# Two query heads mixed in one product in the sliding-window layer of a two-layer decoder

## The chip, the core and the metric

The kernel runs on one core of a Trainium2 chip. The core has a matrix engine (TensorE, PE in the profile; its weight loads are a row of their own, PEld), a vector engine (VectorE, DVE), a scalar engine (ScalarE, ACT), GpSimd (POOL) and a queue that issues transfers (SyncE, SP). Products of PE land in PSUM, which here is used as eight banks of 128 x 512 numbers of 32 bits; ACT and DVE read them from there. The metric is the device time in microseconds of one execution of the whole program: the median over runs, with a profiled execution beside it.

## What is computed

The reference is a decoder trunk of two layers over 512 tokens of width 1024. Layer A is multi-head latent attention with a squared-ReLU MLP; layer B, which the change touches, is sliding-window attention with 16 query heads that share 4 key and value heads, learned sinks and a bias by distance, again with an MLP. Cut to layer B's attention:

```python
def _swa(x, w_q, sinks, w_o, k_band, v_band, rel_bias):
    q = (x @ w_q).reshape(B, nb, BLOCK, SWA_KV_HEADS, G, SWA_HEAD_DIM)
    s = jnp.einsum('bnqkgd,bnjkd->bnkgqj', q, k_band).astype(jnp.float32) * SWA_HEAD_DIM ** -0.5
    ...
    s = jnp.where(mask[None, :, None, None], s + bias, -jnp.inf)
    ...
    m = jnp.maximum(s.max(-1), sink)
    p = jnp.exp(s - m[..., None])
    denom = p.sum(-1) + jnp.exp(sink - m)
    p = (p / denom[..., None]).astype(x.dtype)
    o = jnp.einsum('bnkgqj,bnjkd->bnqkgd', p, v_band).reshape(B, S, SWA_Q_HEADS * SWA_HEAD_DIM)
    return o @ w_o
```

The window is 128 tokens and tokens are handled in 4 blocks of 128, so the queries of a block see the keys of their own block and of the one before: 256 keys, and 128 for the first block.

## The kernel before, in words

**Numbers in two parts.** Each 32-bit number is split into a high part that the fast product format holds exactly and a low rest (`split`, L75: an ACT copy makes the high part at L77, a subtraction on DVE or on another engine makes the low one at L80). Most products are three matmuls: high by high, high by low, low by high (`three`, L108). Where a head is only 64 wide, the high part stands in 64 of the 128 rows and the low part in the other 64, and one matmul does both. `group` (L102) issues such a list into one PSUM bank, so nearly all matmuls carry line L104. PE instructions, and the transfers of SP, are kept in program order (`pe`, L85). Where the instructions of ACT, DVE and POOL stand in their queues, and which PSUM bank or buffer a tile gets, is settled by the framework when the program is built.

**PSUM.** `bank()` (L66) hands out one of 6 banks for products, `tbank()` one of 2 for transposes. A bank comes free when all that reads it is done.

**The steps of layer B.** `run_steps` (L508) walks over the 16 heads. In step u it issues, in this order: the scores of head u + 2 (`AHEAD_B` is 2), pieces of filling work, the turning of head u, and then `mix`, here that of head u - 1 (per 1, lag 1, L1327).

- `scores` (L1224): 8 matmuls into two banks; DVE adds the bias and takes the maximum in four pieces (L1247), turns that into the exponent's offset (L1251); ACT makes four exponentials (L1255) and that of the sink (L1259); DVE sums and inverts; POOL scales the weights `p` (L1262, L1264). The two banks stay taken until the exponentials have read them, the first bank until the second exponential, the second until the fourth.
- filling work: half of a product of queries (`queries`, L1204: 12 matmuls of 512 columns, one bank for the two halves of a pair of heads; evacuated into `q` by ACT at L1218 and DVE at L1219), or a part of the output product w_so (`proj.part`, L457: 6 matmuls of 512 columns; the three token blocks each hold a bank of their own until the product is finished). In steps 1 to 10 a step has one half product of queries: odd steps begin one and take a bank, even steps end it. The list at L1317 gives for each part of w_so its token block t, its piece kp of the sum and the step u in which it is issued.
- `turn` (L1267): 7 transposes of `p` into two transpose banks (L1275, L1277), split into `pth` and `ptl`, of which two buffers each exist.
- `mix` (L1288): the values times the turned weights, for the 4 key blocks, high and low: 8 matmuls, six of 256 columns and two of 128, into one bank. The bank's upper 64 rows hold what the low part of the values gives: ACT copies them to `low` (L1304), DVE adds them to the lower 64 rows into one half of `o` (L1305). After the second head of a pair the pair's `o` is split into `oh` (ACT) and `ol` (POOL), which the output product reads.

After the last step `run_steps` issues what is left of the filling work and the last mix; then `proj.finish` (L467) issues the parts of w_so that are not done, in the order of kp and then t, and the second half of the output columns with the layer norm. The second layer's MLP follows.

Which work stood in which step follows from the list and the shares of filling work in `run_steps` (S scores, Q query half, so(t,kp) part of w_so, T turn, M mix):

```
step 9:  S11 Q T9 M8            step 13:  S15 so(1,0) T13 M12
step 10: S12 Q T10 M9           step 14:  so(1,1) so(2,0) T14 M13
step 11: S13 so(0,0) so(0,1) T11 M10   step 15:  so(2,1) so(0,2) T15 M14
step 12: S14 T12 M11            end:      so(1,2) M15, then finish
```

Of the kernel before, what the change touches and what calls it, by code (L numbers as in the profile page):

```python
# [15 lines left out]
P = 128  # L16
# [32 lines left out]
def build(tc, nc, io, out):  # L49
    with ExitStack() as top:  # L50
# [456 lines left out]

        def run_steps(units, ahead, scores, turn, mix, fill, per, lag, rest):  # L508

            total = sum(f[0] for f in fill)
            n, spent, at = len(units), 0.0, 0
            for u in range(-ahead, n):
                if u + ahead < n:
                    scores(*units[u + ahead])
                target = total * (u + ahead + 1) / (n + ahead)
                while at < len(fill) and (spent < target or fill[at][1] <= u) and fill[at][2] <= u:
                    fill[at][3]()
                    spent += fill[at][0]  # L520
                    at += 1
                if u < 0:
                    continue
                turn(*units[u])
                if u >= lag and (u - lag) % per == per - 1:
                    mix(units[u - lag][0])
            for f in fill[at:]:
                f[3]()
            for f in rest:
                f()  # L530
            for u in range(n, n + lag):
                if (u - lag) % per == per - 1:
                    mix(units[u - lag][0])

# [630 lines left out]
        with tc.tile_pool(name="swa", bufs=1) as mp:  # L1165
# [55 lines left out]
            ps_of = [None] * SQH  # L1221
            pts = [None] * SQH

# [43 lines left out]
            def turn(h, _):  # L1267
                p = ps_of[h]
                pth = mp.tile([P, NT, 256], F32R, tag="pth", bufs=2, name=nm("pth"))
                ptl = mp.tile([P, NT, 256], F32R, tag="ptl", bufs=2, name=nm("ptl"))  # L1270
                for k2 in range(2):
# [8 lines left out]
                    else:  # L1280
                        flat = lambda z: z.rearrange("p a b -> p (a b)")
                        c = slice(512, 512 + 384)
                        split(flat(pth)[:, c], flat(ptl)[:, c], flat(pt)[:, 0:384])
                pts[h] = pth, ptl

            ob = [None] * 8

            def mix(h):  # L1288
                m, a, j = h // 2, h % 2, h // GRP
                if a == 0:  # L1290
                    ob[m] = mp.tile([P, S], F32, tag="o", bufs=2, name=nm("o"))
                o = ob[m]
                pth, ptl = pts[h]

                b = bank()
                for kb in range(NT):
                    w = 256 if kb + 1 < NT else P
                    group(
                        b[:, kb * P : kb * P + w],
                        [(vv[:, kb, j, :], pth[:, kb, :w]), (vv[:, kb, j, :], ptl[:, kb, :w])],  # L1300
                        kb == 0, kb == NT - 1, skip_group_check=True,
                    )
                low = mp.tile([64, S], F32, tag="low", bufs=2, name=nm("low"))
                nc.scalar.activation(low, b[hi, :], AF.Copy)  # L1304
                nc.vector.tensor_add(o[(lo, hi)[a], :], b[lo, :], low)  # L1305
                if a == 1:
                    split(oh[m // 4][:, m % 4, :], ol[m // 4][:, m % 4, :], o, nc.gpsimd)

            proj = TokMajor(Pair(oh, ol), add_scaled_last, "w_so")
            fill = []  # L1310
            for m in range(2, 8):
                for part in range(2):
                    fill.append((2.6, 2 * m - AHEAD_B - 3 + part, -9, lambda m=m, part=part: queries(m, part)))
                if m == 2:
                    for t in range(1, NT):
                        fill.append((2.6, 0, -9, lambda t=t: values(t)))
            for t, kp, u in ((0, 0, 11), (0, 1, 11), (1, 0, 13), (1, 1, 14), (2, 0, 14), (2, 1, 15), (0, 2, 15), (1, 2, 16)):  # L1317
                fill.append((1.3 if t < 2 else 0, u, u, lambda t=t, kp=kp: proj.part(t, kp)))
# [7 lines left out]
            values(0)  # L1326
            run_steps([(h, 0) for h in range(SQH)], AHEAD_B, scores, turn, mix, fill, 1, 1, [])  # L1327

# [116 lines left out]
```

## Time and profile before

| | |
|---|---|
| median of 3 runs | 1007.86 us (1007.84 to 1008.55) |
| the profiled execution's own time | 1009.88 us |
| its span in the profile | 1008.0 us |
| mean granted PE clock over the span | 0.996 |
| busy share of the span: PE, PEld, DVE, ACT, POOL | 98%, 89%, 76%, 55%, 21% |

The profile's times are those of one execution, from the start of its span. A row of a view by groups gives an engine, a line of the kernel, the operation, the tile written and the tiles read, the shape, the count, busy time and the mean length of one. A row of the timeline gives the start, the length, the engine and the instruction; in square brackets stands how long the engine had been idle and what ended that. Matmuls overlap, so that the distance of two starts, and not the length of one, is what a matmul costs; the names of the two operands in a matmul's row do not follow a fixed order. The chain of waits is followed back from the last instruction. Layer B's attention runs from about 521 us to 650 us of the span.

### The profile page before, as it was taken

What the parts mean: (1) busy time and instruction counts of PE and PEld (TensorE: products, weight loads), DVE (VectorE), ACT (ScalarE), POOL (GpSimd) and SP (SyncE); (2) the same over time, 40 slices, a digit from 0 to 9 for tenths busy, and PEclk for the clock granted to TensorE, in tenths of its full rate; (3) what the DMA queues carried; (4) which work ended last, traced back from release to release, by engine and by line L of the source; (5) the groups of instructions that cost most, each with busy time, mean ns of one, the idle gap of its engine ahead of it and who ended that gap; (6) DMA issues with size and microseconds to landing.
All of it is one profiled execution on the core that took longest, in us unless ns stands there. A gap on an engine that the chain in (4) does not pass through costs nothing.

```text
span 1008.0 us, 15943 instructions
## 1 busy us (share of the span) xinstructions
PE 991.8 (98%) x6172; PEld 895.1 (89%) x6172; DVE 770.6 (76%) x1236; ACT 555.0 (55%) x851; POOL 216.1 (21%) x203
## 2 busy tenths in 40 slices
PE   8999999999999999999999999999999999999997
PEld 8888888998999999998899988889898999998986
DVE  5588866998669768877686778698886886898756
ACT  5456653457537637646146688446663754665620
POOL 0231101122212211310003664212122032122000
PEclk9999999999999999999999999999999999999999
DMA  6431136389978986973232212258697798798432
GB/s 245 135 100 50 63 105 210 92 176 236 165 167 219 178 188 194 228 123 129 80 105 96 84 64 74 84 167 195 179 200 175 167 215 168 168 269 147 108 101 84
DMA packets 60247, 149.56 MB, mean 148 GB/s; under 512 B 5211, under 2 KB 9740, under 8 KB 60172
## 3 DMA queue, kind: packets, MB, share of 16 engines
q0 software_dynamic: 24320, 58.73, 33.0%
q1 hardware_dynamic: 35852, 89.82, 26.4%
q8 instruction: 49, 0.80, 0.3%
q14 instruction: 26, 0.21, 0.1%
HBM read 146.41 MB, written 4.22 MB: 149 GB/s over the span
## 4 chain that ended last, share of the span: by engine, by line
PE 95%; ACT 2%; DVE 1%; DMA 1%; issue 1%; SPq 0%; DVEq 0%; ACTq 0%
PE mm L104 87%; PE tr L104 5%; DMA xraw<-in_xT 1%; PE tr L1105 1%; PE tr L647 1%; ACT p L1255 1%; ACT wh L77 1%; PE tr L1275 1%; PE tr L1277 0%; PE tr L427 0%; ACT q L1218 0%; DVE fac L80 0%; ACT pth L77 0%; PE mm L1035 0%; PE tr L899 0%
## 5 line engine op out<-in xcount | busy, mean ns | idle before, releaser
L104 PE MATMUL mm<-wh,fac 128*128 128x512 f32 (+1 forms) x944 | 293.0, 387 | 2.4 <-DVE fac L80 2.3
L77 ACT ACTIVATE wh<-wq 128x1024 fp32r<-128x1024 f32 x164 | 173.5, 1060 | 193.6 <-PE mm L104 135.8
L80 DVE TENSOR_TENSOR wl<-wq,wh 128x1024 fp32r<-128x1024 f32 x164 | 199.5, 1220 | 74.2 <-ACT wh L77 73.4
L104 PE MATMUL mm<-xth,wh 128*128 128x256 f32 (+1 forms) x944 | 246.8, 289 | 0.7 <-ACT p L1255 0.7
L104 PE MATMUL mm<-xth,wl 128*128 128x256 f32 (+1 forms) x816 | 236.1, 289 | 0.0
L104 PEld LDWEIGHTS mm<-wh,fac 128*128 128x128 f32 x944 | 176.1, 188 | 39.0 <-DVE fac L80 3.8
L104 PE MATMUL mm<-xtl,wh 128*128 128x256 f32 (+1 forms) x688 | 199.9, 291 | 0.0
L104 PE MATMUL mm<-wl,fac 128*128 128x512 f32 (+1 forms) x472 | 182.3, 386 | 0.0
L104 PEld LDWEIGHTS mm<-xth,wh 128*128 128x128 f32 x944 | 171.7, 192 | 4.0 <-ACT p L1255 1.5
L104 PEld LDWEIGHTS mm<-xth,wl 128*128 128x128 f32 x816 | 156.3, 192 | 2.0
L77 ACT ACTIVATE wh<-raw 128x1024 fp32r<-128x1024 f32 (+4 forms) x85 | 84.8, 998 | 97.6 <-PE mm L104 65.0
L104 PEld LDWEIGHTS mm<-xtl,wh 128*128 128x128 f32 x688 | 131.8, 192 | 2.4
L199 POOL DMA_DIRECT2D wq<-in_up x64 | 77.5, 1228 | 262.0 <-DVE wl L80 192.1
L80 DVE TENSOR_TENSOR wl<-raw,wh 128x1024 fp32r<-128x1024 f32 (+3 forms) x65 | 76.8, 1188 | 37.7 <-ACT wh L77 37.6
L104 PEld LDWEIGHTS mm<-wl,fac 128*128 128x128 f32 x472 | 88.8, 188 | 16.7
L199 POOL DMA_DIRECT2D wq<-in_down x48 | 42.0, 875 | 188.3 <-DVE wl L80 181.2
L80 POOL TENSOR_TENSOR wl<-raw,wh 128x1024 fp32r<-128x1024 f32 (+2 forms) x20 | 41.4, 2075 | 86.4 <-ACT wh L77 83.9
L104 PE MATMUL mm<-wh,oh 128*128 128x512 f32 x128 | 51.0, 399 | 0.9 <-ACT p L1255 0.9
L104 PE MATMUL mm<-wh,ol 128*128 128x512 f32 x128 | 50.3, 393 | 0.0
L104 PE MATMUL mm<-wl,oh 128*128 128x512 f32 x128 | 50.1, 391 | 0.0
L387 POOL TENSOR_TENSOR rs<-mv,half 128x1 f32<-128x1 f32 x16 | 10.0, 623 | 168.6 <-DVE mv L408 168.5
L553 DVE TENSOR_TENSOR x<-mm,x 128x512 f32<-128x512 f32 (+1 forms) x49 | 32.9, 674 | 15.5 <-PE mm L104 15.5
(217 smaller groups left out, 1847.2 us busy)
## 6 DMA issues: line engine op xcount, KB each, us to landing
wq<-in_up POOLq DMA_DIRECT2D x64, 512.0 KB, 8.5
wq<-in_down POOLq DMA_DIRECT2D x48, 512.0 KB, 6.3
wq<-in_up SPq DMA_DIRECT2D x32, 512.0 KB, 7.1
raw<-in_down SPq DMA_DIRECT2D x28, 512.0 KB, 6.8
wq<-in_down SPq DMA_DIRECT2D x24, 512.0 KB, 5.9
raw<-in_up SPq DMA_DIRECT2D x16, 512.0 KB, 4.8
raw<-in_w_o SPq DMA_DIRECT2D x8, 512.0 KB, 4.1
raw<-in_w_sq SPq DMA_DIRECT2D x8, 512.0 KB, 3.3
```

What stands on the lines that cost most here:

```text
L77: high = nc.scalar.activation(dst_h, src, AF.Copy)
L80: low = (engine or nc.vector).tensor_sub(dst_l, src, f32(dst_h))
L104: pe(nc.tensor.matmul(dst, st, mv, start=first and i == 0, stop=last and i == len(pairs) - 1, **kw))
L199: nc.gpsimd.dma_start(half(a, jp), chunk(*more, jp), accum_op=ALU.add)
L387: nc.gpsimd.tensor_tensor(r, v, half, ALU.pow)
L553: nc.vector.tensor_add(xs[t][:, c], b, xs[t][:, c])
L647: pe(nc.tensor.transpose(pt[:, a, :], xs[t][:, k * P : (k + 1) * P], ident))
L1105: pe(nc.tensor.transpose(pt[:, kb * P : (kb + 1) * P], p[:, kb * P : (kb + 1) * P], ident))
L1255: nc.scalar.activation(p[:, n, lo_c:], bs[n // 2][:, n % 2, lo_c:], AF.Exp, bias=nb[:, n : n + 1], scale=SWA_SCALE, accum_out=sm[:, n : n ...
L1275: pe(nc.tensor.transpose(pt[:, a, 0:P], p[:, kb, P:256], ident))
```

## The change

In layer B the unit of mixing becomes the pair of heads. The turned weights of both heads of a pair stand side by side in one tile, `[P, 2, NT, 256]`, for `pth` and for `ptl`, with one buffer each in place of two of half the size. `mix` handles the pair at once, for two halves of the tokens: for the first 256 tokens key blocks 0 and 1, for the last 256 key blocks 1, 2 and 3, with the columns of both heads in one matmul: 512 columns where it was 256 per head, 256 where it was 128. Key block 1 is cut in two at the token half. Each half has its own bank, in which the two heads lie side by side, its own ACT copy, and two additions on DVE, one for each head. `run_steps` is told per 2 and lag 1, so that a mix stands in every even step from 2 on and one after the last step, and `mix_first`, by which it stands ahead of the turning in its step. Layer A calls `run_steps` as before, without `mix_first`.

The list of parts of w_so is another one. By the same rules as above the steps become:

```
step 9:  S11 Q T9               step 13:  S15 so(1,0) so(1,1) T13
step 10: S12 Q M(8,9) T10       step 14:  so(0,2) so(1,2) M(12,13) T14
step 11: S13 so(0,0) T11        step 15:  so(2,0) so(2,1) T15
step 12: S14 so(0,1) M(10,11) T12   end:  so(2,2) M(14,15), then finish
```

```diff
-        def run_steps(units, ahead, scores, turn, mix, fill, per, lag, rest):
+        def run_steps(units, ahead, scores, turn, mix, fill, per, lag, rest, mix_first=False):
+            def mixes(u):
+                if u >= lag and (u - lag) % per == per - 1:
+                    mix(units[u - lag][0])
...
+                if mix_first:
+                    mixes(u)
                 turn(*units[u])
-                if u >= lag and (u - lag) % per == per - 1:
-                    mix(units[u - lag][0])
+                if not mix_first:
+                    mixes(u)
...
             for u in range(n, n + lag):
-                if (u - lag) % per == per - 1:
-                    mix(units[u - lag][0])
+                mixes(u)
...
-            pts = [None] * SQH
+            pts = [None] * (SQH // 2)
...
-                pth = mp.tile([P, NT, 256], F32R, tag="pth", bufs=2, name=nm("pth"))
-                ptl = mp.tile([P, NT, 256], F32R, tag="ptl", bufs=2, name=nm("ptl"))
+                if h % 2 == 0:
+                    pts[h // 2] = [
+                        mp.tile([P, 2, NT, 256], F32R, tag=tag, bufs=1, name=nm(tag)) for tag in ("pth", "ptl")
+                    ]
+                pth, ptl = (z[:, h % 2] for z in pts[h // 2])
...
             def mix(h):
-                m, a, j = h // 2, h % 2, h // GRP
-                if a == 0:
-                    ob[m] = mp.tile([P, S], F32, tag="o", bufs=2, name=nm("o"))
-                o = ob[m]
-                pth, ptl = pts[h]
-
-                b = bank()
-                for kb in range(NT):
-                    w = 256 if kb + 1 < NT else P
-                    group(
-                        b[:, kb * P : kb * P + w],
-                        [(vv[:, kb, j, :], pth[:, kb, :w]), (vv[:, kb, j, :], ptl[:, kb, :w])],
-                        kb == 0, kb == NT - 1, skip_group_check=True,
-                    )
-                low = mp.tile([64, S], F32, tag="low", bufs=2, name=nm("low"))
-                nc.scalar.activation(low, b[hi, :], AF.Copy)
-                nc.vector.tensor_add(o[(lo, hi)[a], :], b[lo, :], low)
-                if a == 1:
-                    split(oh[m // 4][:, m % 4, :], ol[m // 4][:, m % 4, :], o, nc.gpsimd)
+                m, j = h // 2, h // GRP
+                o = mp.tile([P, S], F32, tag="o", bufs=2, name=nm("o"))
+                for i, blocks in enumerate((((0, 0, 256), (1, 0, P)), ((1, P, 256), (2, 0, 256), (3, 0, P)))):
+                    b = bank().rearrange("p (a b) -> p a b", a=2)
+                    for kb, c0, c1 in blocks:
+                        at = kb * P + c0 - i * 256
+                        group(
+                            b[:, :, at : at + c1 - c0], [(vv[:, kb, j, :], z[:, :, kb, c0:c1]) for z in pts[m]],
+                            kb == i, kb == 2 * i + 1, skip_group_check=True,
+                        )
+                    low = mp.tile([64, 2, 256], F32, tag="low", bufs=2, name=nm("low"))
+                    nc.scalar.activation(low, b[hi, :, :], AF.Copy)
+                    for a, rows in enumerate((lo, hi)):
+                        nc.vector.tensor_add(o[rows, i * 256 : (i + 1) * 256], b[lo, a, :], low[:, a, :])
+                split(oh[m // 4][:, m % 4, :], ol[m // 4][:, m % 4, :], o, nc.gpsimd)
...
-            for t, kp, u in ((0, 0, 11), (0, 1, 11), (1, 0, 13), (1, 1, 14), (2, 0, 14), (2, 1, 15), (0, 2, 15), (1, 2, 16)):
+            for t, kp, u in ((0, 0, 11), (0, 1, 12), (1, 0, 13), (1, 1, 13), (0, 2, 14), (1, 2, 14), (2, 0, 15), (2, 1, 15), (2, 2, 16)):
...
-            run_steps([(h, 0) for h in range(SQH)], AHEAD_B, scores, turn, mix, fill, 1, 1, [])
+            run_steps([(h, 0) for h in range(SQH)], AHEAD_B, scores, turn, mix, fill, 2, 1, [], True)
```

2 lines of the change are left out of this document (removed).

## The prediction, made before the changed kernel was seen

> **What bounds the kernel now.** I read the page first (shares, chain), then the chain and PE's timeline in layer B, and the windows and groups there for what could take PE's place.
>
> ```profile
> PE 95%; ACT 2%; DVE 1%; DMA 1%; issue 1%; SPq 0%; DVEq 0%; ACTq 0%
> ```
>
> PE carries 95% of the chain, so the change is worth what it takes from PE's queue: products, and PE's waits. The chain over one pair of heads shows the wait of a middle step:
>
> ```profile
> 586.78 4.41 PE mm L104 x27
> ...
> 591.21 0.68 ACT wh L77
> ...
> 592.29 0.59 ACT q L1218
> 592.88 0.23 ACT pth L77
> 593.11 0.15 issue
> 593.26 0.91 ACT p L1255 x4
> ```
>
> An odd step's filling part wants a bank; it starts at 594.21, when ACT has made the second exponential of the head before; ACT came to it through a weight split, a query copy and a turned copy. The same rows of PE's timeline show what it costs, and what matmuls cost:
>
> ```profile
> 587.50 0.27 PE L104 MATMUL mm<-skh,q 128*128 128x128 f32 x1
> 588.72 0.40 PE L104 MATMUL mm<-xtl,wh 128*128 128x512 f32 x1
> 591.01 0.39 PE L104 MATMUL mm<-xth,wl 128*128 128x512 f32 x1
> 592.12 0.28 PE L104 MATMUL mm<-ptl,vv 128*128 128x256 f32 x1
> 592.72 0.22 PE L104 MATMUL mm<-pth,vv 128*128 128x128 f32 x1
> 592.89 0.27 PE L104 MATMUL mm<-skh,q 128*128 128x128 f32 x1
> 593.75 0.28 PE L104 MATMUL mm<-skl,q 128*128 128x256 f32 x1
> 594.21 0.50 PE L104 MATMUL mm<-xth,wh 128*128 128x512 f32 x1 [0.18 <-ACT p L1255]
> 594.55 0.39 PE L104 MATMUL mm<-xtl,wh 128*128 128x512 f32 x1
> ```
>
> From start to start: ten of 512 columns take 591.01 - 588.72 = 2.29, **0.229 us** each; five of 256 take 592.72 - 592.12, **0.12** each; the two of 128 take 0.17, **0.085** each. The wait: 594.21 comes 0.46 after a matmul that takes 0.12, and the next start 0.34 after one that takes 0.23: 0.34 + 0.11 = **0.45 us**. The chain shows this wait at 571.76, 582.98, 594.21, 605.45 and 616.67, in steps 3 to 11, once in a pair: 2.25 us.
>
> Steps 12 and 13, where step 12 has no filling work, are worse:
>
> ```profile
> 621.18 0.27 PE L104 MATMUL mm<-skh,q 128*128 128x128 f32 x1
> 624.21 0.28 PE L104 MATMUL mm<-skl,q 128*128 128x256 f32 x1
> 625.31 0.39 PE L104 MATMUL mm<-skh,q 128*128 128x256 f32 x1 [0.83 <-DVE o L1305]
> 625.53 0.28 PE L104 MATMUL mm<-skl,q 128*128 128x256 f32 x1
> 625.77 0.28 PE L104 MATMUL mm<-skl,q 128*128 128x256 f32 x1
> 626.74 0.50 PE L104 MATMUL mm<-wh,oh 128*128 128x512 f32 x1 [0.69 <-ACT p L1255]
> 627.07 0.40 PE L104 MATMUL mm<-wl,oh 128*128 128x512 f32 x1
> ```
>
> Head 15's scores wait for a bank until the addition into `o` (1.10 from start to start, less 0.12: 0.98, and 0.10 behind it), then so(1,0) until an exponential (0.97 - 0.12 = 0.85, and 0.10): **2.03 us**. Right behind follows this, in windows (length, busy us and count of PE, PEld, DVE, ACT, POOL, then PE's granted clock):
>
> ```profile
> 587.00:598.20 11.20, 11.02 (x72) 9.71 (x71) 8.63 (x30) 9.56 (x30) 7.30 (x6) 1.00 0.21 76
> 624.40:627.80 3.40, 1.88 (x10) 1.43 (x10) 3.19 (x10) 3.35 (x13) 1.82 (x2) 1.00 0.01 2
> 627.80:631.20 3.40, 3.40 (x16) 3.11 (x15) 1.88 (x9) 2.06 (x6) 2.73 (x3) 0.50 0.00 0
> ```
>
> For 3.40 us in which PE was busy 1.88 the clock was full, and for the next 3.40 it was half: **1.7 us** lost. ACT, in a middle pair, is busy 9.56 of 11.20 us, DVE 8.63: neither is the bound, but both are queues full enough to be late.
>
> **Products.** A pair costs 12 x 0.12 + 4 x 0.085 = 1.78 us before. After, key blocks 0 and 2 are 4 matmuls of 512 columns, key block 1 is 4 of 256 as before, key block 3 is 2 of 256: 4 x 0.229 + 6 x 0.12 = 1.64. That is 0.14 a pair, and 8 pairs give **-1.15 us** (48 matmuls and as many weight loads fewer). Most of it is key block 3 (0.34 to 0.24). No row shows a moving operand of two stretches; I price it by columns, and the bound from the other side is two 256s for one 512, which leaves -0.8.
>
> [...]
>
> **Evacuation.** Per pair ACT still makes two copies of 64 x 512; DVE makes four additions of 64 x 256 for two of 64 x 512.
>
> ```profile
> L1305 DVE TENSOR_TENSOR o<-mm,low 64x512 f32<-64x512 f32 x15 | 10.2, 680 | 1.0 <-ACT low L1304 0.4 <-issue 0.3
> L1304 ACT ACTIVATE low<-mm 64x512 f32<-64x512 f32 x15 | 9.0, 597 | 0.9 <-PE mm L104 0.5
> L1174 DVE TENSOR_TENSOR skl<-mm,skh 64x256 fp32r<-64x256 f32 x16 | 6.4, 418 | 0.2
> ```
>
> That is 4 x 0.418 - 2 x 0.680 = +0.31 us of DVE a pair (8.63 to 8.94 of about 11): hidden behind PE, priced 0, and it moves the release of the banks below by 0.16 each. Single buffers of `pth` and `ptl` cost nothing: the mix that reads them is issued ahead of the transposes that are then copied over them.
>
> **Banks in the middle steps.** This decides. PE's order over a pair is now: scores 0.99 (592.89 to 593.87), query half 12 x 0.229 = 2.75, turn 0.77, scores, query half, mix 1.64, turn. The odd step is 4.51 us long and the even one 6.15, where each was 5.4. When the odd step starts, six banks hold: even-step scores 2, the finished queries 1, the mix 2, free 1. It wants three: two for scores, one for its part. Before, a mix held one. But the even step's scores are now older: 6.15 + 0.47 = 6.6 us when the second bank for scores is wanted, 6.15 + 0.99 = 7.1 when the part wants its own. How long such a bank is held, from ACT's timeline of the scores that began at 587.50:
>
> ```profile
> 593.61 0.47 ACT L1255 ACTIVATE p<-mm,nb 128x256 f32<-128x256 f32 x1
> 594.50 0.47 ACT L1255 ACTIVATE p<-mm,nb 128x256 f32<-128x256 f32 x1
> ```
>
> The first bank is free after 594.08 - 587.50 = 6.6 us, the second after 7.5. So scores just pass and the part waits 0.35, with 0.11 behind it 0.46: as before, **0**. Bounds: the mix's or the queries' bank comes free sooner, and no wait is left (-2.25); or ACT takes one `low` (0.60) ahead of the exponentials, and 0.6 more is waited in each of five pairs (+3.1). I take 0, since the rows of the same queue give it.
>
> **The last steps.** Step 12 now has so(0,1) and a mix: 0.99 + 1.38 + 1.64 + 0.77 = 4.8 us, no longer 2.6; step 13 has two parts ahead of its turn. The bank demands: the second bank of M(10,11), 6.2 us after scores 13 began; the second bank for scores 15 and one for so(1,0), 5.25 and 5.75 us after scores 14. What they get:
>
> ```profile
> 615.35 0.27 PE L104 MATMUL mm<-skh,q 128*128 128x128 f32 x1
> 621.83 0.49 ACT L1255 ACTIVATE p<-mm,nb 128x256 f32<-128x256 f32 x1
> 626.13 0.46 ACT L1255 ACTIVATE p<-mm,nb 128x256 f32<-128x256 f32 x1
> ```
>
> Scores 13 (615.35) freed their first bank after 7.0 us, scores 14 (621.18) after 5.4, the second 0.9 later. Against the demands: 0.4 (between 0 and 0.8), 0.2, and 0.4: about 1.0 where 2.03 was: **-1.0 us** (bounds -2.0, all hidden, and +0.5). No 3.4 us then hold 1.5 of idle time, so the half-clock stretch goes: **-1.7** in an execution that has it. The first part of each kp also sets off the transfer, ACT split and low part of a later piece of weights; for kp 1 that goes from step 11 to 12, for kp 2 from 15 to 14. No wait of PE here ends on a transfer, and the DMA engines are busy 0.00 to 0.01 in the windows above: 0. Were the piece late, PE would wait at least for its split, 1.06 us by the last row below. so(2,2) moves ahead of the last mix; behind it three parts (4.14) and k = 6 (0.69), and a high pass of k = 7 (0.46), 5.3 us, must hide the way to the last `ol`:
>
> ```profile
> 642.58 0.27 PE L104 MATMUL mm<-ptl,vv 128*128 128x128 f32 x1
> 645.99 1.81 POOL L80 TENSOR_TENSOR ol<-o,oh 128x512 fp32r<-128x512 f32 x1 [6.48 <-ACT oh L77]
> ```
>
> From the end of the mix (642.58 + 0.085) to 647.80 it took 5.1, with DVE's 0.16 5.3: **0**, with no slack left; what is late next is the part (0,3) of the output product, up to +0.5.
>
> **The sum** on the profiled execution: 1009.88 - 1.15 + 0 - 1.0 - 1.7 + 0 = 1006.0 (around its span of 1008.0 lie 1.9). The three runs shown lie 2.02 under that execution, and agree within 0.7: I take it that they do not hold the half-clock stretch, which is 1.7 of the 2.02. So for the median: 1007.86 - 1.15 - 1.0 = **1005.7 us**.
>
> **Rivals.**
> - *The lows stand ahead of the exponentials.* The two copies of a mix come together, right behind a query half that ACT also evacuates; in each odd step scores and part then wait for ACT. From one `low` ahead: +3.1, from two +6.2, and nothing gained in the last steps, which run through the same queue: 1007.86 - 1.15 + 3.1 to 6.2 = 1009.8 to 1012.9, about **1011.4**. It decides from 0.23 us a pair on (1.15 / 5). For: ACT 9.56 of 11.20 busy, and already the last releaser. Against: in an even step 1.52 us of ACT's time went idle ahead of the weight split.
> - *Only the products count:* the waits in the last steps move to other banks at the same price: 1007.86 - 1.15 = **1006.7**. For: six banks, and a mix that wants two at once. Against: step 12 is no longer short.
> - *All waits go:* the extra 0.77 of turning between query half and next scores, and older banks, cover them: 1007.86 - 1.15 - 2.25 - 2.03 = **1002.4**. For: the wait is 0.34 and scores are 0.7 older. Against: two banks of the mix are young.
> - *The products do not get shorter:* two stretches stream worse than a whole operand, say 0.12 more for each of 32 + 48 matmuls: +9.6 - 1.0, **1016**. No row speaks for it.
> - *A half-clock stretch stays in or comes into the runs:* 1005.7 + 1.7 = **1007.4**. The row for it is the one above, at 1.5 us idle of 3.4. [...]
>
> ```profile
> 591.21 1.06 ACT L77 ACTIVATE wh<-raw 128x1024 fp32r<-128x1024 f32 x1 [1.52 <-PE mm L104]
> ```
>
> This row is the idle time of ACT named above.
>
> **How the numbers follow.** Forecast 0.41, all waits go 0.18, lows ahead 0.19, only the products 0.13, half clock 0.06, worse products 0.03. A run tells about 0.2%, 2.0 us, from no change. Faster than 1005.84: all of the second case and somewhat over half of the forecast, whose own range is 1004 to 1007.5: 0.43. Slower than 1009.88: most of the lows, and the worse products: 0.20. Same: 0.37. For 8 in 10 the range goes from 1002.2, past the case without waits, to 1010.4, into that of the lows.
>
> **What would show it.** Products: a pair's ten matmuls with about 1.5 us from the first start to the last, with 0.23 behind those of 512; a start to start of 0.3 or more there makes the step wrong. Middle: in odd steps one wait of 0.3 to 0.5 us that ends on an exponential; two waits, ended by the addition into `o` or by `low`, would be the first rival. Last steps: PE's idle time in 610 to 640 under 1.5 us in all and the granted clock 1.00. End: no idle time ahead of (0,3). I am wrong if the median is above 1009.9 or under 1002.

## The result, and the profile after

| | before | after |
|---|---|---|
| median | 1008.49 us (1007.84 to 1009.90, 5 runs) | 1018.75 us (1016.62 to 1019.87, 5 runs) |
| the profiled execution's own time | 1009.88 us | 1019.04 us |
| its span | 1008.0 us | 1017.3 us |
| mean granted PE clock | 0.996 | 0.992 |

The ratio is 1.0101, with a 95% interval of 1.0090 to 1.0113: the changed kernel is slower by 10.3 us, and was predicted at 1005.7.

The page of the kernel after, share of the chain of waits by engine:

```profile
PE 90%; DVE 4%; DMA 2%; ACT 2%; issue 1%; SPq 0%; DVEq 0%; ACTq 0%
```

PE had 95% of the chain and DVE 1%. PE has lost five points and DVE has won three: something on DVE now stands in PE's way. What PE waits for from 500 to 700 us of the span, first in the kernel before and then after (engine and line that wait, what for, us in total, times, the longest):

```profile
PE mm L104 <- ACT p L1255: 1.6, 6, 0.7
PE mm L104 <- DVE o L1305: 0.8, 1, 0.8
```

```profile
PE tr L1286 <- DVE ptl L80: 11.2, 6, 3.1
```

Both rows of before, which are waits for banks of products, are gone, and a wait of another kind stands in their place: transposes that wait for the low parts `ptl` of transposes made earlier. PE's timeline of the kernel after has the six places:

```profile
574.73 0.30 PE L1286 MATMUL tr<-ident,p 128*128 128x128 f32 x1 [1.72 <-DVE ptl L80]
587.70 0.30 PE L1286 MATMUL tr<-ident,p 128*128 128x128 f32 x1 [2.23 <-DVE ptl L80]
601.75 0.30 PE L1286 MATMUL tr<-ident,p 128*128 128x128 f32 x1 [1.71 <-DVE ptl L80]
614.74 0.30 PE L1286 MATMUL tr<-ident,p 128*128 128x128 f32 x1 [2.24 <-DVE ptl L80]
628.77 0.30 PE L1286 MATMUL tr<-ident,p 128*128 128x128 f32 x1 [3.05 <-DVE ptl L80]
639.92 0.30 PE L1286 MATMUL tr<-ident,p 128*128 128x128 f32 x1 [0.21 <-DVE ptl L80]
```

These are the turns of the odd steps 3, 5, 7, 9, 11 and 13; the even steps have none. Counted from start to start, each costs about 0.16 us more than the idle time shown: the last matmul ahead of the one at 601.75 starts at 599.65 and is worth 0.229, so 2.10 - 0.23 = 1.87 us were lost, where 1.71 stands in the brackets. The six are 12.1 us.

The chain of waits of the kernel after tells how one of them comes about (start, length, what):

```profile
596.35 0.47 PE mm L104 x4
...
596.85 0.31 DVE mm L1254 x2
...
597.77 0.68 DVE q L1226
598.45 0.35 DVE mm L1254 x2
...
598.83 0.42 DVE o L1311
...
600.12 0.42 DVE o L1311
600.54 0.34 DVE mm L1254 x2
...
600.91 0.70 DVE ptl L80
601.62 0.14 issue
601.75 0.30 PE tr L1286
```

Read it backwards. The odd turn (601.75) needs a transpose bank which the even turn (595.43 to 596.35) filled and which is free only when `ptl` has been taken from it (600.91). Ahead of that subtraction DVE's queue holds the four reductions of the next scores (L1254), a query subtraction, and the four additions of the mix (L1311, 598.83 to 600.54). DVE's own timeline, and below it ACT's, speak for a matter of order more than of load:

```profile
596.85 0.30 DVE L1254 CUSTOM_DVE_ANT_0 mm<-mm,bias 128x128 f32<-128x128 f32 x1 [4.80 <-PE mm L104]
598.83 1.71 DVE L1311 TENSOR_TENSOR o<-mm,low 64x256 f32<-64x256 f32 x4
600.91 1.16 DVE L80 TENSOR_TENSOR ptl<-tr,pth 128x512 fp32r<-128x512 f32 x2
```

```profile
597.22 1.08 ACT L1309 ACTIVATE low<-mm 64x512 f32<-64x512 f32 x2
598.32 0.98 ACT L77 ACTIVATE pth<-tr 128x512 fp32r<-128x512 f32 x2
```

DVE had stood idle for 4.80 us until the scores came, and then worked without a pause for as long, with `ptl` last. The same order stands ahead of the four other long waits. The input of `ptl`, the first `pth`, was there from about 598.9, itself behind the two copies `low` in ACT's queue. From the start of the even turn to the end of the first `ptl` pass 601.61 - 595.43 = 6.2 us, to the end of the second 602.07 - 595.43 = 6.6. The same in the kernel before, by PE's and DVE's timelines from 591 to 598 us:

```profile
591.24 0.27 PE L1275 MATMUL tr<-ident,p 128*128 128x128 f32 x1
...
597.09 0.27 PE L1275 MATMUL tr<-ident,p 128*128 128x128 f32 x1
...
597.52 0.27 PE L1275 MATMUL tr<-ident,p 128*128 128x128 f32 x1
```

```profile
593.63 0.69 DVE L80 TENSOR_TENSOR ptl<-tr,pth 128x512 fp32r<-128x512 f32 x1
...
596.07 0.53 DVE L80 TENSOR_TENSOR ptl<-tr,pth 128x384 fp32r<-128x384 f32 x1
```

The first `ptl` ended 3.1 us after its turn began, 2.8 us before the next turn wanted the bank; the second, which frees the bank that the fifth transpose wants (597.52), ended 5.4 us after it, with 0.9 us to spare. And there were 5.85 us from turn to turn. After the change they would be 4.45 without the wait (the even turn at 595.43, the matmul ahead of the odd one over at 599.88), since the mix of every second step went ahead of the even turn. So the release came 3.1 us later for the first bank and was due 1.4 us earlier: the 2.8 us to spare became a wait of 1.7.

**The balance of the two profiled executions.** Layer B's attention, from the first matmul on `skh` to the last on `w_quadb`, a piece of the MLP's weights behind it, by the rows of these tiles (among their columns the first and last start), before and after:

```profile
L104 PE MATMUL mm<-skh,q x64: 220/282/386, 542.0 to 625.7; 128*128 128x256 f32 x48, 128*128 128x128 f32 x16
L104 PE MATMUL mm<-xth,w_quadb x32: 278/283/363, 196.9 to 687.5; 128*128 128x256 f32 x32
```

```profile
L104 PE MATMUL mm<-skh,q x64: 220/305/527, 540.9 to 636.6; 128*128 128x256 f32 x48, 128*128 128x128 f32 x16
L104 PE MATMUL mm<-xth,w_quadb x32: 278/283/363, 195.8 to 696.1; 128*128 128x256 f32 x32
```

That is 145.5 us and 155.2: +9.7, which is all the difference (own times: +9.2). New waits +12.1, old waits -4.3 (2.25 and 2.03), products -1.15, half clock +3.4 (three stretches for one, below) make about +10.0.

### The profile page after: what moved, and what is told of

Its sections match the earlier page's. It is cut to its first block, busy times and chain, and to the rows that moved or that the text cites. A ratio compares the mean times of both kernels' runs of the same rounds, so it can differ in the third digit from the quotient of the medians.

```text
span 1017.3 us, 15855 instructions
## 1 busy us (share of the span) xinstructions
PE 992.3 (98%) x6124; PEld 892.8 (88%) x6124; DVE 774.1 (76%) x1252; ACT 555.2 (55%) x851; POOL 217.1 (21%) x203
## 4 chain that ended last, share of the span: by engine, by line
PE 90%; DVE 4%; DMA 2%; ACT 2%; issue 1%; SPq 0%; DVEq 0%; ACTq 0%
PE mm L104 83%; PE tr L104 4%; DVE o L1311 1%; DMA wq<-in_up 1%; ACT wh L77 1%; PE tr L1286 1%; PE tr L1112 1%; PE tr L654 1%; DVE mm L1254 1%; DVE wl L80 1%; DMA xraw<-in_xT 1%; PE tr L1288 0%; DMA raw<-in_down 0%; DVE ptl L80 0%; DVE fac L80 0%
```

## The experiments

The theory after the result (queue theory in the expectations): DVE's queue holds two demands of PE, the subtractions `ptl` that free the transpose banks and the reductions that let the exponentials free the score banks. The changed order puts four additions and four reductions ahead of `ptl`, in a step too short for it. Rivals: the wide products themselves; the new list of w_so; the mix ahead of the turn alone; the load of DVE and not its order (load theory); the short odd step whatever the order (step theory). In the diffs `with behind(x)` puts what is issued inside it after the instructions x in its engine's queue, and `split(...)[1:]` is the subtraction that makes the low part.

| kernel | median, us | before, us | ratio, 95% interval | what PE waits for, 521 to 720 us |
|---|---|---|---|---|
| new_list | 1008.60 | 1009.32 | 0.9993 (0.9983 to 1.0002) | `p` 1.6 |
| first_only | 1011.70 | 1008.55 | 1.0031 (1.0020 to 1.0042) | `ptl` 3.1, `pth` 1.2 |
| old_list | 1016.05 | 1009.32 | 1.0069 (1.0047 to 1.0090) | `ptl` 9.5 |
| one_head_products | 1017.99 | 1008.71 | 1.0089 (1.0074 to 1.0105) | `ptl` 9.1 |
| adds_twice | 1035.86 | 1009.32 | 1.0259 (1.0234 to 1.0285) | `ptl` 18.6 |
| adds_behind | 1011.76 | 1008.55 | 1.0030 (1.0020 to 1.0039) | `ptl` 3.4, `p` 1.1 |
| reduce_behind | 1012.32 | 1008.55 | 1.0041 (1.0026 to 1.0056) | `ptl` 3.2, `p` 2.1, `o` 1.9 |
| both_behind | 1023.88 | 1009.32 | 1.0142 (1.0123 to 1.0160) | `p` 9.3, `ptl` 3.9 |
| half_behind | 1029.55 | 1008.92 | 1.0198 (1.0180 to 1.0216) | `o` 8.3, `oh` 2.1, `ptl` 1.9, `ol` and `q` 1.4 each |
| mix_behind | 1017.50 | 1008.55 | 1.0094 (1.0077 to 1.0111) | `ptl` 6.1, `ol` 2.0 |
| turn_later | 1014.84 | 1008.71 | 1.0061 (1.0047 to 1.0076) | `o` 5.7 |
| exp_first | 1013.21 | 1008.71 | 1.0045 (1.0032 to 1.0057) | `ptl` 5.2, `p` 1.6 |

"Before" is the kernel before, run beside each. The waits are of one profiled execution each, those over 1.0 us that tell most.

### Which part of the change costs

**new_list:** the kernel before with the new list of w_so alone.

```diff
-            for t, kp, u in ((0, 0, 11), (0, 1, 11), (1, 0, 13), (1, 1, 14), (2, 0, 14), (2, 1, 15), (0, 2, 15), (1, 2, 16)):
+            for t, kp, u in ((0, 0, 11), (0, 1, 12), (1, 0, 13), (1, 1, 13), (0, 2, 14), (1, 2, 14), (2, 0, 15), (2, 1, 15), (2, 2, 16)):
```

> The kernel before with the new steps of the parts of w_so alone; products and mixes are one head's. If the steps of w_so are worth what the prediction gave them in the last steps (2.0 us of waits to 1.0, and no half-clock stretch): 1006 to 1007.5. If step 11, which loses a part, is the next short step: the same waits one step earlier, 1008.5.

No difference that can be told: the interval holds 1. So the list by itself does no harm. Whether it brings the 1.0 us that the prediction gave it stays open, since the interval goes from 1.7 us faster to 0.2 slower. In its profile the wait of 0.8 us for `o` is gone and one of 0.6 for a `ptl` in step 11 stands in its place.

**first_only:** the kernel before, one head to a mix, with the mix ahead of the turn.

```diff
+                if mix_first:
+                    mixes(u)
                 turn(*units[u])
-                if u >= lag and (u - lag) % per == per - 1:
-                    mix(units[u - lag][0])
+                if not mix_first:
+                    mixes(u)
...
-            run_steps([(h, 0) for h in range(SQH)], AHEAD_B, scores, turn, mix, fill, 1, 1, [])
+            run_steps([(h, 0) for h in range(SQH)], AHEAD_B, scores, turn, mix, fill, 1, 1, [], True)
```

> The kernel before with one thing changed: the mix of one head stands ahead of the turn in its step; products, steps of w_so and the number of additions are those of before. Every step is 5.4 us long. Queue theory: one addition of 0.68 us and the reductions may stand ahead of ptl, but 4.6 us of cover lie between turns: waits of 0 to 0.5 us, 1007 to 1011. Step theory: as before, 1008.5. If the place of the mix were enough to lose the time: 1015 or more.

Slower by 3.2 us, just above the 1007 to 1011 of the queue theory. PE's waits for `ptl` in this kernel:

```profile
PE mm L104 <- DVE ptl L80: 3.1, 7, 1.0
```

They stand in another place than expected: here no transpose waits but the mix itself, seven times, for a `ptl` that is due earlier by the turn which used to stand between. So moving the mix makes `ptl` due earlier in any case; with pairs the price is paid at the transpose banks and is over three times as large.

**old_list:** the changed kernel with the list of before (the diff of new_list, turned round).

> The changed kernel with the old steps of the parts of w_so. Queue theory: the five waits in steps 3 to 11 are the same, 8 to 10 us; in steps 12 and 13 the short step 12 adds to them: 1018 to 1021. If the new list were what costs the time: 1010.

Five waits for `ptl`, up to 2.2 us long, are there, so the list is not the cause. The time lies below the 1018 to 1021 that were expected and 2.7 us below that of the changed kernel; the intervals (1.0047 to 1.0090 and 1.0090 to 1.0113) touch. In the profiled executions most of the difference is the clock: one half-clock stretch in layer B's attention here, three in the changed kernel, 3.4 us (last section), and a mean granted clock of 0.997 against 0.992. The rest would be the sixth wait and a longer fifth one there.

**one_head_products:** the changed kernel's steps and tiles, with the matmuls, copies and additions of before, one head at a time.

```diff
-                for i, blocks in enumerate((((0, 0, 256), (1, 0, P)), ((1, P, 256), (2, 0, 256), (3, 0, P)))):
-                    b = bank().rearrange("p (a b) -> p a b", a=2)
+                for a in range(2):
+                    b = bank()
+                    for kb in range(NT):
+                        w = 256 if kb + 1 < NT else P
...
+                            b[:, kb * P : kb * P + w], [(vv[:, kb, j, :], z[:, a, kb, :w]) for z in pts[m]],
...
-                    for a, rows in enumerate((lo, hi)):
-                        nc.vector.tensor_add(o[rows, i * 256 : (i + 1) * 256], b[lo, a, :], low[:, a, :])
+                    low = mp.tile([64, S], F32, tag="low", bufs=2, name=nm("low"))
+                    nc.scalar.activation(low, b[hi, :], AF.Copy)
+                    nc.vector.tensor_add(o[(lo, hi)[a], :], b[lo, :], low)
```

> The changed kernel's steps (a pair mixed in each even step, ahead of the turn), but with the products and additions of one head each as in the kernel before: 16 matmuls and two additions of 64 x 512 (1.36 us) for a pair in place of 10 and four of 64 x 256 (1.71 us). Queue theory: the loss lies in the steps and not in the products, so waits of 1.5 to 2.9 us stay at the odd turns, 0.35 less each for the shorter additions, and the products cost 1.15 more: 1017 to 1019. If the products of two heads were what loses (two stretches, four additions): 1009 to 1011.

```profile
PE tr L1286 <- DVE ptl L80: 9.1, 6, 2.3
```

As expected (1017 to 1019), the loss is all there without the wide products, and with two long additions in place of four short ones. It comes with mixing a pair at a time in every second step, not with how the products are made.

### Is it the place in DVE's queue

**adds_twice:** each of the four additions made twice, and kept ahead of the first `ptl` of the turn.

```diff
+                        with behind(added[:1] if added[0] else None):
+                            split(pth[:, 0:2, :], ptl[:, 0:2, :], pt)
...
-                        nc.vector.tensor_add(o[rows, i * 256 : (i + 1) * 256], b[lo, a, :], low[:, a, :])
+                        for _ in range(2):
+                            added[0] = nc.vector.tensor_add(o[rows, i * 256 : (i + 1) * 256], b[lo, a, :], low[:, a, :])
```

> The changed kernel with each addition of a mix made twice (the second writes the same numbers), and the first ptl subtraction of the even turn put behind the last of the eight. In VectorE's queue then stand ahead of that ptl four more additions (1.7 us), a query subtraction (0.69) and the second ptl (0.54): 2.9 us more than in the changed kernel. Queue theory: PE pays all of it in each of six odd turns, +15 to 17 us and more where the clock falls, 1034 to 1040. Load theory (VectorE's sum of work, 1.7 us a pair more of about 13): about +1.7 a pair, 1030, with the waits spread over other places. Step theory: nothing said about the sum; the wait stands at the odd turn.

Slower by 26.5 us, in two runs, and in the range of the queue theory (1034 to 1040), but not made up as it said. It let PE pay 2.9 us more in each of six turns; the idle time for `ptl` grew by 7.4 us in all, and the mean granted clock of the profiled execution is 0.983 where the changed kernel's is 0.992: over the spans of 1035.5 and 1017.3 us that is about 17.6 us lost against 8.1, 9.5 more. So the waits grow with what stands ahead of `ptl`, but not by all of it; and as this run adds work too, it cannot tell order from load. The waits have become twelve, five of the turns with one for each of the two banks:

```profile
PE tr L1288 <- DVE ptl L80: 18.6, 12, 3.4
```

**adds_behind:** the changed kernel, PE's order and all arithmetic as they are; the two copies and four additions of a mix are issued after the turn, and the additions stand behind its `ptl`.

```diff
-                        split(flat(pth)[:, c], flat(ptl)[:, c], flat(pt)[:, 0:384])
+                        turned[0] = split(flat(pth)[:, c], flat(ptl)[:, c], flat(pt)[:, 0:384])[1:]
+                with behind(turned[0]):
+                    flush()
...
+                    late.append(lambda i=i, b=b: out_half(i, b))
+                def out_half(i, b):
...
-                split(oh[m // 4][:, m % 4, :], ol[m // 4][:, m % 4, :], o, nc.gpsimd)
+                late.append(lambda: split(oh[m // 4][:, m % 4, :], ol[m // 4][:, m % 4, :], o, nc.gpsimd))
```

> The changed kernel, but in VectorE's queue the four additions of a mix stand behind the ptl subtractions of the turn that follows the mix; PE's order is the same. Queue theory (in the changed kernel the odd turn waits for the transpose banks, which ptl sets free, and ptl stands behind the next scores' reductions and the four additions, 1.7 us): the six waits of 0.4 to 3.2 us, 12.1 us in all, shrink by about 1.7 each to 0 to 1, the half-clock stretches go with them, and the median is about 1007. Load theory (VectorE has too much to do, in whatever order): the waits stay in sum, 1018. Step theory (the odd step is too short for the evacuation of the turn before it, whatever the order): waits of 1 us or more stay in odd steps, 1013 or more.

```profile
PE tr L1288 <- DVE ptl L80: 3.4, 5, 1.1
PE mm L104 <- ACT p L1264: 1.1, 2, 0.9
```

```profile
598.54 0.69 DVE L80 TENSOR_TENSOR ptl<-tr,pth 128x512 fp32r<-128x512 f32 x1
...
600.46 1.70 DVE L1318 TENSOR_TENSOR o<-mm,low 64x256 f32<-64x256 f32 x4
```

This is the run that carries the theory: with nothing moved but instructions in the queues behind PE, the loss falls from 10.3 us to 3.2 and the wait for `ptl` from 11.2 to 3.4. The additions now stand behind `ptl` (the last rows), while ACT still makes the two copies ahead of `pth`, so it is DVE's order that counts. DVE's load is the same, which speaks against the load theory. Part of the gain is the clock: none of the three half-clock stretches is left in layer B's attention (5.1 us in the profiled executions; the mean granted clock is 0.996 where it was 0.992). It does not bring the kernel under the one before, and misses the 1007 that were expected by 4.8 us: five waits of 0.5 to 1.1 us stay at the odd turns.

**reduce_behind:** the reductions of the next scores behind `ptl` instead, additions as in the changed kernel.

```diff
-                        nc.vector.tensor_tensor_reduce(
+                        with behind(turned[0]):
+                            nc.vector.tensor_tensor_reduce(
```

> The changed kernel, but in VectorE's queue the reductions of the next scores stand behind the ptl subtractions of the turn issued ahead of them; the additions stay ahead of ptl. Queue theory: ptl no longer waits for scores that PE makes later, VectorE does not sit idle ahead of them (4.8 us in the changed kernel), the waits fall below 0.5 each, about 1007. Were it the additions alone and not the reductions, half of the waits would stay, 1012. Load theory: 1018. Step theory: 1013 or more.

```profile
PE tr L1289 <- DVE ptl L80: 3.2, 5, 1.3
PE mm L104 <- ACT p L1265: 2.1, 3, 0.7
PE mm L104 <- DVE o L1314: 1.9, 1, 1.9
```

The other half of what stood ahead of `ptl` gives nearly as much: 3.8 us slower than before, where about 1007 was expected. The 1012 that the text gave for additions alone is met in number, but not by its sign: 3.2 us of waits for `ptl` are left and not half of them, and 4.0 us of waits for banks have come, which are the price of this order.

### Can both demands be met

**both_behind:** the two diffs above together.

> The changed kernel with both orders in VectorE's queue: the reductions of the next scores behind ptl, and the additions behind ptl. Queue theory: ptl is first of the three, the waits at the turns go to about 0; what is late next is the exponentials, since the reductions stand behind 1.2 us of ptl: waits of 0.5 to 1 at the bank for scores, 1008 to 1011. Step theory: waits of 0.5 or more stay at the odd turns, 1011 to 1013.

The expectation failed, by some 13 us. PE's waits of this kernel, and one of the places in its timeline:

```profile
PE mm L104 <- ACT p L1265: 9.3, 10, 1.7
PE tr L1289 <- DVE ptl L80: 3.9, 6, 1.3
```

```profile
596.51 0.39 PE L104 MATMUL mm<-pth,vv 128*128 128x256 f32 x1 [1.68 <-ACT p L1265]
```

```profile
DVE ptl L80 <- ACT pth L77: 12.9, 13, 3.0
```

The second bank of five mixes now waits 1.5 to 1.7 us for the exponentials, since the reductions of two heads come in a lump behind `ptl` and the additions, and the exponentials after them. It is the bank wait that the prediction had weighed, made real by the cure for the other one. And with `ptl` first in its queue DVE itself waits 12.9 us for ACT's `pth` (the last row, of DVE's waits), while the reductions stand behind: 3.9 us of PE's waits for `ptl` remain.

**half_behind:** in between: of an odd head's scores the last two reductions stand behind `ptl`, and the additions behind the exponent's offset.

```diff
+                        with behind(turned[0] if n2 and h % 2 == 1 else ()):
+                            nc.vector.tensor_tensor_reduce(
...
+                base = nc.vector.tensor_scalar(nb, mx, sink8[:, h : h + 1], -SWA_SCALE, ALU.max, ALU.mult)
+                if h % 2:
+                    with behind((base,)):
+                        flush()
```

> The kernel with the additions behind the even turn's ptl, and besides: of the odd head's next scores, the last two of the four reductions on DVE stand behind that ptl, and the additions only behind the exponent's offset that these reductions give. So DVE's order in an odd step is: two reductions, ptl of the even turn, two reductions, offset, additions. If DVE's queue has a place for all three (the queue alone matters): ptl no longer waits for the second bank of scores, the waits of PE for ptl fall from 3.4 us to under 1.5, the exponentials are late by about one ptl (0.5 us), bank waits on them under 1.5 us in all: 1008 to 1010. If two demands compete and each place given to one is taken from the other: what leaves the waits on ptl comes back as waits for banks that the exponentials or the additions hold, 0.5 to 1 us in each of six pairs: 1011 to 1014.

```profile
PE mm L104 <- DVE o L1323: 8.3, 5, 1.8
```

Worse than the text had it either way. The wait for `ptl` is down to 1.9 us, and the additions, now last, hold the banks of the mix until the next scores want one: a third demand on the same queue. Six half-clock stretches take another 10.2 us of the profiled execution: the granted clock over 10 us was 0.66 from 590 us on, 0.83 from 620 and from 630, 0.97 from 640 and 0.69 from 650.

**turn_later:** adds_behind, with the odd turn moved behind the next step's scores, which gives the even `ptl` a longer way.

```diff
+                if mix_first and u > 0 and u % 2 == 0:
+                    turn(*units[u - 1])
...
-                turn(*units[u])
+                if not mix_first or u % 2 == 0:
+                    turn(*units[u])
```

> The kernel adds_behind (the changed kernel with the additions behind ptl) with the odd turn moved behind the next step's scores, so that the turns follow each other after 4.7 and 4.4 us and not after 3.7 and 5.4. Step theory (what is left in adds_behind, 0.4 to 0.85 us at each odd turn, comes from the short odd step): these waits go, 1008 to 1009. Queue theory alone: a turn that is later makes ptl later for the mix, 2.75 us behind it, and the exponentials of the next scores want a third weights buffer that is not free: waits of 0.5 to 1 us move to the mix, 1011 to 1014.

```profile
PE mm L104 <- DVE o L1323: 5.7, 6, 3.2
```

The waits for `ptl` are gone from the turns, as meant, and the scores, not the mix as expected, wait for banks that the additions hold. 1014.84 us is just above the 1011 to 1014 of the queue theory; the step theory alone (1008 to 1009) is out.

**mix_behind:** the changed kernel without `mix_first`: the pair's mix behind the turn.

```diff
-            run_steps([(h, 0) for h in range(SQH)], AHEAD_B, scores, turn, mix, fill, 2, 1, [], True)
+            run_steps([(h, 0) for h in range(SQH)], AHEAD_B, scores, turn, mix, fill, 2, 1, [])
```

> The changed kernel without mix_first: the pair's products come behind the even turn, so that 5.4 us and not 3.7 lie between the even turn and the odd one. Queue theory: with 1.6 us more cover the waits of the odd turns fall to about 0.5 each, others may come at the even turn or at the bank for scores: 1008 to 1011. Step theory: the waits of odd turns are gone, and with them all the loss, 1005. Load theory: 1018.

This missed the 1008 to 1011 of the queue theory, and its number is the 1018 of the load theory, which adds_behind speaks against. The waits at the turns are about half as large (6.1 us), but now the last mix's `ol` is late for the output product. Over its own runs of before it is 9 us slower, as far as the intervals tell the same as the changed kernel. At the wait that ends at 611.15 DVE's queue holds the four reductions, two of the additions and a query subtraction ahead of `ptl` (610.32) here too. That `pth` and `ptl` have one buffer each was not the hold there: the last matmul on them started at 605.63, and ACT made the next `pth` at 608.12. So moving the mix back does not give `ptl` its place in the queue; what each of the other waits comes from was not followed up.

**exp_first:** the kernel before with the new list, and ACT's splits of weights placed behind the exponentials: an attempt to get the old 0.45 us waits without the pairs.

```diff
-                    with behind((state["norm"],) if after else None):
+                    with behind((state["norm"],) if after else state.get("exp")):
...
-                nc.scalar.activation(ri, nb, AF.Exp, bias=sink[:, h : h + 1])
+                state["exp"] = (nc.scalar.activation(ri, nb, AF.Exp, bias=sink[:, h : h + 1]),)
```

> The kernel before with the new steps of w_so (new_list) and one order in ScalarE's queue: a weight split whose transfer is asked for in layer B's steps stands behind the exponentials of the scores issued last. In the kernel before the bank wait of each pair came from ScalarE standing at the weight split until PE set its buffer free (1.52 us), the exponentials behind it. If that is the cause of the 0.45 us waits, they go in all five pairs: -2.25 us against new_list, 1006.3. If the exponentials are late for another reason (the reductions on VectorE), nothing moves: 1008.6. If the late weight split is wanted at once: slower, 1010.

```profile
PE tr L1275 <- DVE ptl L80: 5.2, 5, 2.6
```

It missed, and is 4.5 us slower than before: the regular waits for `p` are gone (one of 1.6 us is left), and waits for `ptl` stand in their place in the kernel before too, without pairs. So it seems that the old order, with its small wait in each pair, had been a compromise between the two.

No version found beats the kernel before; new_list equals it.

## Why the prediction was wrong, point by point

**The step that failed** is the pricing of order on DVE. It stands in the prediction in two places: that the 0.31 us more of additions are "hidden behind PE, priced 0", and the part "Banks in the middle steps", which opens with "This decides" and counts only the six banks of products. The two transpose banks were counted nowhere. (That "Single buffers of `pth` and `ptl` cost nothing" the trace of after bears out: no copy over them waits for a mix.) The prediction did work out that the odd step shrinks to 4.51 us and the even one grows to 6.15, and asked what that does to the age of scores; it did not ask what it does to `ptl`, whose two passes had 2.8 and 0.9 us to spare. The 0.31 us of load was about right (four additions take 1.71 us, two took 1.36) and beside the point: what counts is the 1.71 us that the four additions, now in one lump, stand ahead of the release, with the reductions of the next scores, while the next turn comes 1.4 us earlier. The balance has +12.1 us there, where the sum had 0.

**Banks of products, priced 0 with bounds of -2.25 and +3.1.** The waits of 0.45 us went, the end at -2.25. That does not make "all waits go" right: it seems that in the changed kernel the exponentials have time because PE stands still a step later. Where reduce_behind shortened the stops at the turns, three waits of 0.7 us for `p` came back in the middle steps, though that run also makes the reductions later; in adds_behind those for `p` (1.1 us) stand in the last steps.

**Products, -1.15 us.** Right. PE's timeline of the kernel after, a pair's mix from its first matmul to its last:

```profile
606.26 0.39 PE L104 MATMUL mm<-pth,vv 128*128 128x512 f32 x1
606.49 0.39 PE L104 MATMUL mm<-ptl,vv 128*128 128x512 f32 x1
...
607.77 0.28 PE L104 MATMUL mm<-ptl,vv 128*128 128x256 f32 x1
```

From 606.26 to 607.77 are 1.51 us, as the text had it, and with 0.12 for the last one 1.63 (1.64 predicted). An operand of two stretches, one for each head, costs 0.23 us as a whole one does; that rival is out. In the whole kernel the 1.15 us can't be told: the intervals of the changed kernel and of one_head_products overlap.

**The last steps, -1.0 us.** The 2.03 us of before are gone, but the turns of steps 11 and 13 wait 3.21 and 0.37 us from start to start in their place, the largest wait of all among them. What the list is worth by itself new_list could not tell.

**Half clock, -1.7 us.** Wrong in sign: three stretches where there was one, behind the new waits of 2.23, 2.24 and 3.05 us (last section). The prediction had read the one of before next to the 3.40 us ahead of it, in which PE was busy 1.88. Its sum took it for something that only goes away, and the rival in which a stretch comes in had one of them, at 1.7 us, and did not tie it to new waits.

**The end, 0.** Right: from 639 to 700 us PE's only idle time on a semaphore is 0.2 us, again for a `ptl` (the last of the six); nothing is waited for ahead of (0,3).

**The rivals.** Two forecast a slower kernel. The nearest in number, products that do not get shorter (1016), is out by the rows above. The other, lows ahead of the exponentials (1011.4), named a mechanism that the trace of after does not have: ACT makes the two `low` at 597.22, behind the exponentials, and no bank of products is waited for. The right rival had to be found on DVE: DVE is busy 76% of the span and was on the chain for 1% only.

## What to carry to other kernels

List everything that an engine's queue releases, not only the banks that the change uses more of: in DVE's queue here each released resource had its own due time, and the rows show the slack of each (2.8 and 0.9 us for the two passes of `ptl`, none for the score banks). A change that makes steps uneven spends the slack of the short step (here the 5.85 us from turn to turn would have become 4.45), and gathering small operations into one lump (here four additions, 1.71 us) puts the lump ahead of whatever is next in the queue, though the load hardly changes. When putting one release first makes another one late, as in the last runs here, reordering moves a wait without removing it.

## What the runs showed of the hardware that was not expected

In the kernel after, three half-clock stretches of 3.41 us stand in layer B's attention, each behind a wait that is shorter than the stretch: 2.23, 2.24 and 3.05 us. Windows of this kernel (length, busy us and count of PE, PEld, DVE, ACT, POOL, then PE's granted clock, DMA share, GB/s), each pair the 3.4 us before a stretch and the stretch:

```profile
585.40:588.80 3.40, 1.17 (x11) 1.08 (x11) 3.28 (x9) 1.06 (x2) 1.53 (x2) 0.99 0.20 62
588.80:592.20 3.40, 3.40 (x13) 2.92 (x13) 3.11 (x14) 2.45 (x11) 0.15 (x1) 0.51 0.42 169
612.70:616.10 3.40, 1.36 (x12) 1.35 (x13) 3.29 (x9) 1.32 (x3) 1.27 (x1) 0.99 0.26 89
616.10:619.50 3.40, 3.40 (x12) 2.82 (x11) 2.85 (x13) 2.19 (x10) 0.41 (x2) 0.50 0.76 289
626.40:629.80 3.40, 1.02 (x9) 1.01 (x10) 3.31 (x8) 1.55 (x3) 1.62 (x2) 0.99 0.02 5
629.80:633.20 3.40, 3.40 (x13) 3.01 (x13) 3.17 (x15) 2.52 (x11) 0.06 (x1) 0.51 0.01 2
```

PE was busy 1.0 to 1.4 us of each window before, and never idle for more than 3.05 us at a stretch (the brackets at the turns); each time 3.4 us at half clock followed, 1.7 us lost. The waits of 2.23, 2.24 and 3.05 us are followed by a stretch, those of 1.72 and 1.71 are not; the kernel before had one behind a window with 1.88 us busy and no idle time above 0.83. So PE was busy for part of the 3.4 us ahead of each of these four stretches.

By the granted clock the three stretches begin at 588.75, 616.06 and 629.71: 27.31 and 13.65 us apart. Which waits are followed by a stretch, and why the kernel before has one with so little idle time, these runs do not show. The clock varies from run to run: the five runs of the changed kernel have mean clocks of 0.992 to 0.996, and the fastest has the highest.
